# Gates of a mixing layer computed in a phase of their own, with seven products for eight

## The chip, the cores and the metric

The kernel runs on one core of a Trainium2 chip. Its time is device microseconds of one execution; the kernel before took 3154.03, 3162.03 and 3159.44 us in three runs, median 3159.44. The engines of the core are TensorE (PE; its weight loads are PEld), VectorE (DVE), ScalarE (ACT), GpSimd (POOL), and SyncE (SP), whose queue issues the DMAs in the order in which they stand in it: an issue that waits for a semaphore holds back all that stand behind it.

## The reference, cut to what matters

One decoder layer over 2048 prompt tokens and 64 sample tokens. What the change touches is the mix of three branches, each 512 wide, under gates, and the two norms behind it:

```
h = rms_norm(x, pre_mix_g)                     # 1024 wide
gate_logits = (h @ w_in)[:, 2304:]             # 3 branches x 1024
proj  = einsum('blnc,ncd->blnd', branches, w_o)
mixed = sum_n(sigmoid(gate_logits) * proj)
x1    = x + rms_norm(mixed, post_mix_g)
up    = rms_norm(x1, pre_ffn_g) @ w_up         # 1024 -> 2 x 2816, then conv, gelu, product
y     = x1 + rms_norm(act @ w_down, post_ffn_g)
```

## The kernel before

All tensors stand transposed, channels on the 128 partitions and tokens along the row. A number is kept as two float32r parts, high and low (`split`: an ACT copy, L72, and a DVE subtraction, L73), and a product of two such is three matmuls (high by high, high by low, low by high). Stage 1, to about 720 us, computes the projections and the three branches, which go to DRAM (`br`), and the norm of x by token (`rbc_d`). Stage 2 takes the 2112 tokens in three groups of 704, each of two chunks of 352 columns. It has three phases.

The mix phase (`mix_phase`) is the one that is rebuilt. Per group, `branches` goes over 3 branches x 4 steps; a step loads two tiles of gate weights (`ws_g`, 512 KB each) and one of projection weights (`ws_p`), splits them, and makes two output tiles. For each, `gemm` (L741) runs 48 matmuls for the gate (8 k-tiles x 3 passes x 2 chunks) and 24 for the projection, ACT takes the sigmoid out of PSUM (L872), DVE multiplies it with the projection (L877; L874 in the first branch, whose projections are made ahead by `proj0`), and POOL adds it to the sum (L878). At the end of a group `post_mix` takes the norm of the sum: two small PE chains (`rstd_rows`: ones against the squares, L84; a spread over the partitions, L94) with DVE, POOL and DVE between and behind, then per tile a DVE scaling (L891), a POOL addition of x (L894), a store to `x1_d` and a square, and a second such chain gives the norm of x1 (`rs2_d`). `build_h` then makes the next group's input.

Beside this, 22 calls of `prep`, one after each step, make for the up phase the four sums of weight blocks that a seven-product (Strassen) scheme needs: four loads of 256 KB (`pr`), four DVE sums (L816), four splits (`pw`), four stores of 512 KB to `sum_d`.

The up phase (`up_phase`) has 22 jobs in each of the 3 groups, and each job makes two output tiles of 704 tokens. The 2x2 blocks (two halves of the inner dimension by two output tiles, two halves by two chunks of the tokens) are multiplied with seven products of 12 matmuls each in place of eight: three with plain weight blocks (`ra`, 256 KB each), four with sums (`ws`, 512 KB each, from `sum_d`). The DVE additions that put the products together are L1031. `build_ops` makes the sums and differences of the token blocks. The down phase is not touched.

Instructions are put in order by a scheduler when the kernel is built, by priorities and pools; that order decides what stands behind a waiting instruction.

Of the kernel before, what the change touches and what calls it, by code (L numbers as in the profile page):

```python
# [9 lines left out]
F32 = mybir.dt.float32  # L10
# [5 lines left out]
P = 128  # L16
# [26 lines left out]
def tile_decoder_layer(ctx, tc, I, O):  # L43
# [8 lines left out]
    rs2_d = dpool.tile([P, NTOK], F32, tag="rs2d", name="rs2_d")  # L52
    sum_d = [dpool.tile([4, P, 2, 512], F32, tag=f"sumd{f}", name=f"sum_d{f}") for f in range(NF)]
# [46 lines left out]
    stage2(tc, I, O, br, rbc_d, x1_d, rs2_d, act_d, sum_d, gains, split, PASSES, rstd_rows)  # L100
# [609 lines left out]
def stage2(tc, I, O, br, rbc_d, x1_d, rs2_d, act_d, sum_d, gains, split, PASSES, rstd_rows):  # L710

    nc = tc.nc
    PSUM = bass.MemoryType.PSUM
    with ExitStack() as c2:

        def pool(stack, name, bufs):
            return stack.enter_context(tc.tile_pool(name=name, bufs=bufs, reuse_waits="tile"))

        cm = c2.enter_context(ExitStack())
        hp, wp, lp, sp = pool(cm, "h2", 13), pool(cm, "w2", 4), pool(cm, "ld2", 2), pool(cm, "s2", 2)  # L720

        def psum(stack, name):
            return stack.enter_context(tc.tile_pool(name=name, bufs=3, space=PSUM, reuse_waits="tile"))

        ps2 = psum(cm, "ps2")

        def load_w(src, nm):
            w = wp.tile([P, 2, 1024], F32R, tag="w", name=f"w_{nm}")
            t = lp.tile([P, 1024], F32, tag="ws", name=f"ws_{nm}", bufs=2)
            nc.sync.dma_start(out=t, in_=src)  # L730
            split(w[:, 0], w[:, 1], t)
            return w.rearrange("p s (k c) -> p s k c", c=P)

        def gemm(w, ks, xs, nm, spare=False):

            ps = ps2.tile([P, 2, 512], F32, tag="st" if spare else "mm", name=f"ps_{nm}", bufs=1 if spare else 3)
            n, tot = 0, 3 * len(xs)
            for k, x in zip(ks, xs):
                for a, b in PASSES:
                    for c in range(2):  # L740
                        nc.tensor.matmul(  # L741
                            ps[:, c, :CW], lhsT=w[:, a, k], rhs=x[:, b, c * CW : (c + 1) * CW],
                            start=(n == 0), stop=(n == tot - 1),
                        )
                    n += 1
            return ps[:, :, :CW]

        def v2(t):
            return t.rearrange("p (c n) -> p c n", c=2)

        class SumSq:


            def __init__(self, nm, nt=T2):
                self.nm, self.n, self.nt = nm, 0, nt
                self.acc = sp.tile([P, T2], F32, tag="ac", name=f"ac_{nm}", bufs=2)[:, :nt]

            def add(self, m):
                if self.n == 0:
                    nc.scalar.activation(self.acc, m, AF.Square)  # L760
                else:
                    sq = sp.tile([P, T2], F32, tag="sq", name=f"sq_{self.nm}_{self.n}", bufs=2)[:, : self.nt]
                    nc.scalar.activation(sq, m, AF.Square)
                    nc.vector.tensor_tensor(out=self.acc, in0=self.acc, in1=sq, op=ALU.add)
                self.n += 1

            def rs(self):
                psb = ps2.tile([P, 2, 512], F32, tag="st", name=f"ps_st_{self.nm}", bufs=1)
                _, self.chain = rstd_rows(
                    self.acc, self.nt, psb[:, 0, CW:], lambda c0, w: psb[:, c0 // CW, c0 % CW : c0 % CW + w], sp,  # L770
                    self.nm,
                )
                rs = sp.tile([P, T2], F32, tag="rs", name=f"rs_{self.nm}")
                nb = self.nt // CW
                nc.vector.tensor_copy(
                    out=rs[:, : self.nt].rearrange("p (c n) -> p c n", c=nb), in_=psb[:, :nb, :CW]
                )
                return rs[:, : self.nt]

        env = dict(locals())  # L780
        mix_phase(c2, tc, env)
        cm.close()
        for phase in (up_phase, down_phase):
            with ExitStack() as cs:
                env["ps2"] = psum(cs, "ps_" + phase.__name__)
                phase(c2, tc, env)


def mix_phase(c2, tc, env):

    (nc, I, br, rbc_d, x1_d, rs2_d, sum_d, gains, split, pool, hp, sp, lp, load_w, gemm, v2, SumSq) = (
        env[n] for n in (
            "nc", "I", "br", "rbc_d", "x1_d", "rs2_d", "sum_d", "gains", "split", "pool", "hp", "sp", "lp", "load_w",
            "gemm", "v2", "SumSq",
        )
    )
    with ExitStack() as ca:
        mp, ep, pp_ = pool(ca, "mx2", 13), pool(ca, "e2a", 4), pool(ca, "prep", 2)
        todo = list(range(NF))

        def prep():

            if not todo:
                return
            f = todo.pop(0)
            a = []
            for i in range(4):
                t = pp_.tile([P, 512], F32, tag="r", name=f"pr_{f}_{i}", bufs=4)
                nc.sync.dma_start(out=t, in_=I["w3"][f][:, i * 512 : (i + 1) * 512])
                a.append(t)  # L810
            a11, a12, a21, a22 = a
            for i, (o, p, m, op) in enumerate((
                (a22, a21, a22, ALU.add), (a21, a11, a21, ALU.subtract), (a11, a22, a11, ALU.subtract),
                (a12, a12, a11, ALU.subtract),
            )):
                nc.vector.tensor_tensor(out=o, in0=p, in1=m, op=op)  # L816
                w = pp_.tile([P, 2, 512], F32R, tag="pw", name=f"pw_{f}_{i}")
                split(w[:, 0], w[:, 1], o)
                nc.sync.dma_start(out=sum_d[f][i], in_=_f(w))

        def build_h(g):
            c0 = g * T2
            rb = sp.tile([P, T2], F32, tag="rbx", name=f"rbx_{g}", bufs=1)
            nc.sync.dma_start(out=rb, in_=rbc_d[:, c0 : c0 + T2])
            out = []
            for k in range(KT):
                h = hp.tile([P, 2, T2], F32R, tag="h", name=f"h_{g}_{k}")
                x = lp.tile([P, T2], F32, tag="ld", name=f"hx_{g}_{k}")
                nc.sync.dma_start(out=x, in_=I["xT"][:, k, c0 : c0 + T2])
                nc.vector.scalar_tensor_tensor(  # L830
                    out=x, in0=x, scalar=gains[:, 0, k : k + 1], in1=rb, op0=ALU.mult, op1=ALU.mult
                )
# [459 lines left out]
```

## Time and profile before

| what | value |
|---|---|
| median of three runs | 3159.44 us |
| the profiled execution | 3162.45 us |
| its span | 3160.7 us |
| PE busy in the span | 2996.0 us (95%) |
| DVE, ACT, POOL busy | 1821.8, 1329.4, 547.0 us |
| mean granted TensorE clock | 0.971 |
| moved by DMA | 566.88 MB, mean 179 GB/s |
| mix phase, about 720 to 1648 us | 928 us |

The profiled execution is 3.0 us above the median. Busy shares are means over stages with different limits, so the stages have to be read apart: the windows below do that. In them "DMA share" is the mean busy share of the core's 16 DMA engines, and PEclk is the granted TensorE clock, 1.00 being 2.4 GHz and 0.50 being 1.2 GHz.

### The profile page before, as it was taken

What the parts mean: (1) busy time and instruction counts of PE and PEld (TensorE: products, weight loads), DVE (VectorE), ACT (ScalarE), POOL (GpSimd) and SP (SyncE); (2) the same over time, 40 slices, a digit from 0 to 9 for tenths busy, and PEclk for the clock granted to TensorE, in tenths of its full rate; (3) what the DMA queues carried; (4) which work ended last, traced back from release to release, by engine and by line L of the source; (5) the groups of instructions that cost most, each with busy time, mean ns of one, the idle gap of its engine ahead of it and who ended that gap; (6) DMA issues with size and microseconds to landing.
All of it is one profiled execution on the core that took longest, in us unless ns stands there. A gap on an engine that the chain in (4) does not pass through costs nothing.

```text
span 3160.7 us, 51575 instructions
## 1 busy us (share of the span) xinstructions
PE 2996.0 (95%) x20060; PEld 2950.8 (93%) x20060; DVE 1821.8 (58%) x3061; ACT 1329.4 (42%) x2371; POOL 547.0 (17%) x662
## 2 busy tenths in 40 slices
PE   8999999998999699989994999999999997999997
PEld 8899999998999699979994999999999997999997
DVE  6665766546656832462228665865586655555552
ACT  5555565114333422332213444544454444444441
POOL 3221100000011301130113101311132210222221
PEclk9999999999999799989996999999999998999999
DMA  6222223218787832252217777777777757666652
GB/s 201 62 61 82 88 86 105 64 48 313 261 276 246 295 131 86 88 177 67 72 46 253 250 246 244 266 245 244 240 262 245 240 174 255 219 223 216 208 187 100
DMA packets 245268, 566.88 MB, mean 179 GB/s; under 512 B 30672, under 2 KB 103888, under 8 KB 245008
## 3 DMA queue, kind: packets, MB, share of 16 engines
q1 hardware_dynamic: 245024, 563.59, 53.5%
q8 instruction: 158, 2.59, 0.3%
q14 instruction: 86, 0.70, 0.1%
HBM read 459.35 MB, written 105.13 MB: 179 GB/s over the span
## 4 chain that ended last, share of the span: by engine, by line
PE 78%; DMA 8%; DVE 7%; issue 3%; ACT 2%; POOL 1%; SPq 0%; DVEq 0%; ACTq 0%; POOLq 0%
PE ps_d L1141 16%; PE ps_x L997 16%; PE ps_g L741 11%; PE ps_y L997 8%; PE ps_p L741 4%; PE ps_w L997 4%; PE ps_q L189 3%; PE ps_up L203 3%; PE ps_sv L189 3%; DMA pr<-in_w_dram 3%; PE ps_mqp L203 3%; DMA sum_d<-pw 2%; PE ps_kv L189 1%; DVE m L891 1%; DVE pw L73 1%
## 5 line engine op out<-in xcount | busy, mean ns | idle before, releaser
L741 PE MATMUL ps_g<-h,w_g 128*128 128x352 f32 x3456 | 574.1, 326 | 18.6 <-ACT m L855 18.6
L741 PEld LDWEIGHTS ps_g<-h,w_g 128*128 128x128 f32 x3456 | 566.3, 191 | 19.1 <-ACT m L855 19.1
L1141 PE MATMUL ps_d<-a,wd 128*128 128x352 f32 x3168 | 512.5, 323 | 17.8 <-ACT a L72 17.1
L1141 PEld LDWEIGHTS ps_d<-a,wd 128*128 128x128 f32 x3168 | 508.6, 189 | 19.1 <-ACT a L72 17.7
L741 PE MATMUL ps_p<-b,w_p 128*128 128x352 f32 x1728 | 291.4, 326 | 18.6 <-ACT w_p L72 13.0
L741 PEld LDWEIGHTS ps_p<-b,w_p 128*128 128x128 f32 x1728 | 283.2, 191 | 20.3 <-ACT w_p L72 13.4
L1065 DVE SCALAR_TENSOR_TENSOR c<-e,k_conv_w,c 128x704 f32<-128x704 f32 (+1 forms) x264 | 252.1, 956 | 68.8 <-ACT c L1061 61.7
L73 DVE TENSOR_TENSOR wd<-wr,wd 128x1408 fp32r<-128x1408 f32 x96 | 161.4, 1685 | 206.1 <-ACT wd L72 204.6
L997 PE MATMUL ps_x<-ot,ws 128*128 128x352 f32 x1584 | 277.5, 323 | 0.6 <-ACT p L1006 0.5
L997 PEld LDWEIGHTS ps_x<-ot,ws 128*128 128x128 f32 x1584 | 258.4, 189 | 1.9 <-ACT p L1006 1.0
L73 DVE TENSOR_TENSOR wa<-ra,wa 128x512 fp32r<-128x512 f32 x198 | 134.9, 689 | 155.5 <-ACT wa L72 154.7
L878 POOL TENSOR_TENSOR m<-m,sg 128x704 f32<-128x704 f32 x48 | 98.2, 2045 | 709.6 <-DVE sg L877 495.1
L72 ACT CAST wd<-wr 128x1408 fp32r<-128x1408 f32 x96 | 131.8, 1372 | 109.1 <-PE ps_d L1141 90.7
L872 ACT ACTIVATE sg<-ps_g 128x704 f32<-128x704 f32 x72 | 54.5, 756 | 284.4 <-PE ps_g L741 284.3
L1061 ACT ACTIVATE c<-e,k_conv_b,k_conv_w 128x704 f32<-128x704 f32 (+1 forms) x132 | 129.6, 982 | 68.8 <-DVE e L1031 49.0
L997 PE MATMUL ps_x<-ob,wa 128*128 128x352 f32 x792 | 147.3, 326 | 11.7 <-ACT wa L72 7.4
L72 ACT CAST wa<-ra 128x512 fp32r<-128x512 f32 x198 | 121.8, 624 | 85.9 <-PE ps_y L997 46.2
L73 DVE TENSOR_TENSOR w_g<-ws_g,w_g 128x1024 fp32r<-128x1024 f32 x72 | 98.7, 1371 | 91.9 <-ACT w_g L72 89.3
L1052 POOL COPY tails<-e 128x2 f32<-128x2 f32 x88 | 61.4, 697 | 520.6 <-DVE e L1031 520.4
L997 PE MATMUL ps_w<-ob,wa 128*128 128x352 f32 x792 | 147.9, 323 | 0.7 <-ACT wa L72 0.7
L997 PE MATMUL ps_y<-ot,ws 128*128 128x352 f32 x792 | 146.7, 324 | 0.3 <-DMA ws<-sum_d 0.3
L997 PEld LDWEIGHTS ps_x<-ob,wa 128*128 128x128 f32 x792 | 131.7, 191 | 12.5 <-ACT wa L72 7.6
(304 smaller groups left out, 5037.3 us busy)
## 6 DMA issues: line engine op xcount, KB each, us to landing
ws<-sum_d SPq DMA_DIRECT2D x264, 512.0 KB, 5.1
wr<-in_w_dram SPq DMA_DIRECT2D x96, 704.0 KB, 4.1
ra<-in_w_dram SPq DMA_DIRECT2D x198, 256.0 KB, 3.8
sum_d<-pw SPq DMA_DIRECT2D x88, 512.0 KB, 5.0
ws_g<-in_w_dram SPq DMA_DIRECT2D x72, 512.0 KB, 4.0
af<-act_d SPq DMA_DIRECT2D x132, 176.0 KB, 4.1
pr<-in_w_dram SPq DMA_DIRECT2D x88, 256.0 KB, 5.0
ws_p<-in_w_dram SPq DMA_DIRECT2D x36, 512.0 KB, 3.3
```

Of the source, the lines that this page charges most:

```text
L72: nc.scalar.copy(out=hi, in_=src)
L73: nc.vector.tensor_tensor(out=lo, in0=src, in1=_f(hi), op=ALU.subtract)
L189: nc.tensor.matmul(ps[:nt, :256], lhsT=h[k // 4][:, a, k % 4, c0 : c0 + nt], rhs=wv[:, b, k], start=(n == 0), stop=(n == 3 * KT - 1),)
L203: nc.tensor.matmul(ps[:, :nt], lhsT=wv[:, a, k, half * P : (half + 1) * P], rhs=h[k // 4][:, b, k % 4, :nt], start=(n == 0), stop=(n == 3 ...
L741: nc.tensor.matmul(ps[:, c, :CW], lhsT=w[:, a, k], rhs=x[:, b, c * CW : (c + 1) * CW], start=(n == 0), stop=(n == tot - 1),)
L872: nc.scalar.activation(v2(sg), ps, AF.Sigmoid)
L878: nc.gpsimd.tensor_tensor(out=mx[o], in0=mx[o], in1=sg, op=ALU.add)
L997: nc.tensor.matmul(ps[:, :CW], lhsT=self.ws[w][:, a, j], rhs=self.ops[o][j][:, b], start=(start and n == 0), stop=(n == 3 * HK - 1), skip_ ...
L1052: nc.gpsimd.tensor_copy(out=tails[:, ft], in_=e[:, T2 : T2 + 2])
L1061: nc.scalar.activation(c[:, :cwid], e[:, 2:ew], AF.Identity, bias=cb[:, ft : ft + 1], scale=cw[:, ft, 2:3])
L1065: nc.vector.scalar_tensor_tensor(out=c[:, :cwid], in0=e[:, t : t + cwid], scalar=cw[:, ft, t : t + 1], in1=c[:, :cwid], op0=ALU.mult, op1= ...
L1141: nc.tensor.matmul(ps[:, :CW], lhsT=w[:, a, k], rhs=acts[i * HF + k][:, b], start=(n == 0), stop=(n == 3 * NF - 1),)
```

## The change

The seven-product scheme of the up phase becomes a class, `Strassen`, which two phases use. A new `gate_phase` makes all gates before anything is mixed: per group 12 jobs, each two output tiles (84 matmuls, where two gate `gemm`s took 96). For group 0 the four sums of gate weights are made on DVE and stored to DRAM (12 more entries of `sum_d`); groups 1 and 2 load them. Sigmoids are taken in SBUF and stored (`sg_d`, 352 KB each, 2 per job). The 22 weight preparations for the up phase now follow the jobs of groups 1 and 2 only. The `mix_phase` that is left runs the projections, and loads the sigmoids (`sl`, five buffers). `post_mix` of a group runs inside the next group, and that of the last group after the loop. The squares of x1 are summed and stored (`acx_d`); the up phase loads them and takes the norm itself (`norms`), for group 0 ahead of its first operands, for the others during the group before. The pool for x (`xr`) has two buffers in place of four shared ones.

```
-        mix_phase(c2, tc, env)
-        cm.close()
-        for phase in (up_phase, down_phase):
...
+    for phase in (gate_phase, mix_phase, up_phase, down_phase):
...
 class Strassen:
+        def weights(self, w, sums, first, nm):
...
             for n, i in (("a11", 0), ("s1", 0), ("a12", 1), ("s2", 2), ("s4", 3), ("s3", 1), ("a22", 3)):
+                if first == "sums" and n[0] == "a":
+                    continue
+                t = wo.tile([P, 2, HK * P], F32R, tag="w", name=f"w{n}_{nm}")
+                if n[0] == "a":
+                    split(t[:, 0], t[:, 1], block(i))
+                elif first:
+                    split(t[:, 0], t[:, 1], total(i))
+                    nc.sync.dma_start(out=sums[i], in_=_f(t))
+                else:
+                    nc.sync.dma_start(out=_f(t), in_=sums[i])
...
+        def run(self, jobs):
...
+                p1 = self.copy(q, self.product(q, "x", "a11", "b11", True), "p1")
+                if prev:
+                    self.end(prev)
+                p5 = self.copy(q, self.product(q, "y", "s1", "t1", True), "p5")
+                sink.add(0, 0, p1, self.product(q, "w", "a12", "b21", True))
+                u2 = self.copy(q, self.product(q, "x", "s2", "t2", False), "u2")
+                sink.add(0, 1, u2, self.product(q, "y", "s4", "b22", False))
+                sink.half(0)
+                u3 = self.copy(q, self.product(q, "x", "s3", "t3", False), "u3")
+                sink.add(1, 1, u3, p5)
...
+def gate_phase(c2, tc, env):
...
+    op_, wo, rw = pool(c2, "ops", 32), pool(c2, "wo", 12), pool(c2, "raw", 10)
+    lp, gp, cp = pool(c2, "ldu", 3), pool(c2, "sg", 4), pool(c2, "cp", 8)
...
+        def move(self, h, c, ps):
+            nc.scalar.activation(chunk(self.sg[h], c), ps, AF.Sigmoid)
+        def half(self, h):
+            part = chunk(self.sg[h], 1) if h else self.sg[h]
+            nc.scalar.activation(part, part, AF.Sigmoid)
+            nc.sync.dma_start(out=sg_d[2 * self.i + h][:, self.g * T2 : (self.g + 1) * T2], in_=self.sg[h])
...
+            for i in range(12):
+                yield f"g{g}_{i}", eng.weights(I["wg"][i], sum_d[NF + i], g == 0, f"g{g}_{i}"), ops, Sink(g, i)
+                if g and todo:
+                    f = todo.pop(0)
+                    eng.weights(I["w3"][f], sum_d[f], "sums", f"u{f}")
...
+def mix_phase(c2, tc, env):
...
+                    sg = gp.tile([P, T2], F32, tag="sg", name=f"sl_{g}_{n}_{o}")
+                    nc.sync.dma_start(out=sg, in_=sg_d[8 * n + o][:, g * T2 : (g + 1) * T2])
...
+                if held and n == 0 and op == 1:
+                    post_mix(*held)
+                    held = None
+        held = g, mx, acc
+    post_mix(*held)
...
+    def norms(g):
+        rb = lp.tile([P, T2], F32, tag="rb", name=f"rb2_{g}", bufs=1)
+        acc = ep.tile([P, E_W], F32, tag="e", name=f"acx_{g}")
+        nc.sync.dma_start(out=acc[:, :T2], in_=acx_d[g])
+        for c in range(2):
+            psb = ps2.tile([P, 512], F32, tag="st", name=f"ps_su{g}_{c}", bufs=1)
+            cols = slice(c * CW, (c + 1) * CW)
+            rstd_rows(acc[:, cols], CW, psb[:, CW:], lambda c0, w: psb[:, c0 : c0 + w], kp, f"u{g}_{c}")
+            nc.vector.tensor_copy(out=rb[:, cols], in_=psb[:, :CW])
+        return rb
...
+                if f == 8 and g + 1 < NG2:
+                    rb = norms(g + 1)
```

Two places of SP's queue show what this moves. The first is one gate step. Before, in group 0, `pr` and `pw` are the raw blocks and split sums of a weight preparation, `ws_g` and `ws_p` the weights of gates and projections:

```order
L730 DMA ws_g0_1_30_10373<-in_w2_dram 128x1024
L819 DMA sum_d8_73<-pw_8_0_10775 128x1024
L809 DMA pr_9_0_10971<-in_w3_dram 128x512
L819 DMA sum_d8_73<-pw_8_1_10780 128x1024
L809 DMA pr_9_1_10973<-in_w3_dram 128x512
L819 DMA sum_d8_73<-pw_8_2_10785 128x1024
L809 DMA pr_9_2_10975<-in_w3_dram 128x512
L730 DMA ws_g0_1_31_10378<-in_w2_dram 128x1024
L819 DMA sum_d8_73<-pw_8_3_10790 128x1024
L809 DMA pr_9_3_10977<-in_w3_dram 128x512
L730 DMA ws_p0_1_3_10383<-in_w2_dram 128x1024
```

Now, in group 1 around job 10: `r` is a raw block and `ws` a sum, `u9` and `u10` belong to up-weight preparations, `g1_9` and `g1_10` to gate jobs, and `sg0_1_9` is the first sigmoid tile of gate job 9:

```order
L795 DMA sum_d9_76<-ws1_u9_12504 128x1024
L769 DMA r1_u9_12523<-in_w3_dram 128x512
L876 DMA sg_d18_119<-sg0_1_9_12399 128x704
L795 DMA sum_d9_76<-ws2_u9_12514 128x1024
L769 DMA r0_g1_10_12537<-in_wg_dram 128x512
L769 DMA r1_g1_10_12544<-in_wg_dram 128x512
L769 DMA r3_g1_10_12555<-in_wg_dram 128x512
L769 DMA r2_u10_12665<-in_w3_dram 128x512
L769 DMA r3_u10_12667<-in_w3_dram 128x512
L795 DMA sum_d9_76<-ws4_u9_12522 128x1024
L795 DMA sum_d9_76<-ws3_u9_12530 128x1024
L797 DMA ws1_g1_10_12541<-sum_d32_99 128x1024
```

In groups 1 and 2 a sigmoid store now stands in the queue between the loads of one job and those of the next; `sg0_1_9` is complete when the fifth product of job 9 (`s4`, the order on PE being a11, a12, s1, s2, s4, s3, a22) has been added and put through the sigmoid, and the raw blocks `g1_10` and its sums stand behind it. Before, no issue in this stretch waits for a result of PE.

The second place is the end of the mix. Before, `rb2` is the norm of x1 of group 0, `ux` are tiles of x1 for the up phase's operands, `ra` its raw weight blocks:

```order
L895 DMA x1_d2_111<-m_2_6_14217 128x704
L895 DMA x1_d2_111<-m_2_7_14244 128x704
L944 DMA rb2_0_16440<-rs2_d_64 128x704
L950 DMA ux_0_0_16442<-x1_d0_109 128x704
L950 DMA ux_0_4_16445<-x1_d0_109 128x704
L950 DMA ux_0_1_16477<-x1_d0_109 128x704
L931 DMA k_conv_w_16431<-in_conv_w_dram 128x132
L931 DMA k_conv_b_16433<-in_conv_b_dram 128x44
L931 DMA k_state_16435<-in_state_dram 128x704
L950 DMA ux_0_5_16480<-x1_d0_109 128x704
L897 DMA rs2_d_64<-rs_x12_16396 128x704
```

Now `x_u0` are the same tiles, `acx` are the summed squares:

```order
L744 DMA x_u0_1_17776<-x1_d0_147 128x704
L947 DMA x1_d2_149<-m_2_7_17018 128x704
L949 DMA acx_d2_66<-acx_2_17608 128x704
L1002 DMA k_conv_w_17703<-in_conv_w_dram 128x132
L1002 DMA k_conv_b_17705<-in_conv_b_dram 128x44
L1002 DMA k_state_17707<-in_state_dram 128x704
L769 DMA r0_u0_0_17882<-in_w3_dram 128x512
L769 DMA r1_u0_0_17889<-in_w3_dram 128x512
L769 DMA r3_u0_0_17900<-in_w3_dram 128x512
L769 DMA r0_u0_1_17999<-in_w3_dram 128x512
L769 DMA r1_u0_1_18006<-in_w3_dram 128x512
L1016 DMA acx_0_17713<-acx_d0_64 128x704
```

The load that the norm of group 0 needs, `acx_0`, has moved behind the last store of x1, the store of `acx_2`, three tables and five weight blocks, and the two chains on PE and the copies on DVE follow it; the loaded norm `rb2_0` stood right behind the stores.

On DVE the eight scalings of `post_mix` (L943 after, L891 before) stand in one block in both. In the new order the copy of the norm and the block stand between the products of a sigmoid with the projections 4 and 5 of the next group's first branch.

## Rows read from the trace of the kernel before

**Rows 1.** Windows by stage: from:to, length; busy us (instructions) by engine; PEclk, share, GB/s

```profile
720.00:1010.00 290.00, 277.25 (x1706) 276.08 (x1707) 182.59 (x224) 116.82 (x160) 29.39 (x14) 0.98 0.79 276
1010.00:1110.00 100.00, 67.25 (x392) 66.32 (x391) 81.15 (x89) 44.52 (x62) 29.81 (x12) 0.80 0.82 290
1110.00:1340.00 230.00, 230.00 (x1424) 230.00 (x1424) 76.17 (x73) 58.41 (x70) 29.68 (x15) 1.00 0.29 96
1340.00:1410.00 70.00, 54.48 (x324) 53.90 (x323) 53.60 (x48) 28.06 (x36) 25.15 (x11) 0.84 0.59 195
1410.00:1645.00 235.00, 235.00 (x1457) 235.00 (x1456) 64.03 (x59) 51.09 (x60) 29.83 (x16) 1.00 0.20 66
1645.00:1740.00 95.00, 46.89 (x245) 44.27 (x244) 69.48 (x99) 31.13 (x61) 31.03 (x16) 0.66 0.64 221
1880.00:1920.00 40.00, 40.00 (x252) 40.00 (x251) 23.95 (x33) 19.19 (x34) 3.90 (x12) 1.00 0.74 252
```

**Rows 2.** Chain of waits, inside group 1: start us, us, what

```profile
1165.91 7.76 PE ps_g L741 x48
1173.67 3.88 PE ps_p L741 x24
```

**Rows 3.** Lines by form: operation, xcount | busy us, mean ns | idle before, releasers

```profile
L741 PE MATMUL ps_g<-h,w_g 128*128 128x352 f32 x3456 | 574.1, 326 | 18.6 <-ACT m L855 18.6
...
L73 DVE TENSOR_TENSOR pw<-pr,pw 128x512 fp32r<-128x512 f32 x88 | 65.1, 745 | 37.6 <-ACT pw L72 37.5
...
L872 ACT ACTIVATE sg<-ps_g 128x704 f32<-128x704 f32 x72 | 54.5, 756 | 284.4 <-PE ps_g L741 284.3
...
L1031 DVE TENSOR_TENSOR e<-p,ps_w 128x352 f32<-128x352 f32 x66 | 34.1, 516 | 58.8 <-PE ps_w L997 58.8
```

**Rows 4.** Windows in which the DMA engines are full, columns as in the first group

```profile
720.00:740.00 20.00, 8.54 (x42) 8.54 (x43) 11.34 (x16) 7.29 (x10) 0.00 (x0) 0.66 1.02 363
...
1710.00:1720.00 10.00, 5.39 (x32) 4.81 (x31) 4.98 (x11) 2.14 (x5) 0.00 (x0) 0.92 1.04 406
1730.00:1740.00 10.00, 10.00 (x63) 9.69 (x62) 10.00 (x19) 7.11 (x15) 6.08 (x3) 1.00 1.02 359
```

**Rows 5.** Timeline, mix to up: start us, us, what [idle before <-releaser]

```profile
1643.89 4.04 PE L741 MATMUL ps_p<-b,w_p 128*128 128x352 f32 x24
...
1661.65 15.45 DVE L891 SCALAR_TENSOR_TENSOR m<-m,c_gains,rs_mix 128x704 f32<-128x704 f32 x8
...
1682.56 0.32 SPq L944 DMA_DIRECT2D rb<-rs_d  x1
...
1686.78 2.48 PE L84 MATMUL ps_st_x<-ones,ac_x 128*88 128x1 f32 x16 [26.09 <-DVE ac_x L764]
...
1689.47 1.81 DVE L951 SCALAR_TENSOR_TENSOR ux<-ux,c_gains,rb 128x704 f32<-128x704 f32 x2
...
1695.73 0.89 DVE L775 COPY rs_x<-ps_st_x 128x704 f32<-128x704 f32 x1 [0.54 <-PE ps_st_x L94]
...
1703.07 0.96 PE L997 MATMUL ps_x<-ob,wa 128*128 128x352 f32 x2 [7.38 <-ACT wa L72]
```

**Rows 6.** DMA issues: xcount, KB each, median us from issue to landing

```profile
ws<-sum_d SPq DMA_DIRECT2D x264, 512.0 KB, 5.1
...
ra<-in_w_dram SPq DMA_DIRECT2D x198, 256.0 KB, 3.8
sum_d<-pw SPq DMA_DIRECT2D x88, 512.0 KB, 5.0
...
br<-ob SPq DMA_DIRECT2D x16, 256.0 KB, 2.4
```

**Rows 7.** Timeline around the norm of group 0, columns as in the other timeline

```profile
1068.63 15.55 DVE L891 SCALAR_TENSOR_TENSOR m<-m,c_gains,rs_mix 128x704 f32<-128x704 f32 x8
...
1076.34 13.75 PE L741 MATMUL ps_g<-h,w_g 128*128 128x352 f32 x73 [10.55 <-ACT m L855]
...
1100.29 7.58 PE L741 MATMUL ps_g<-h,w_g 128*128 128x352 f32 x35
```

More of the change, by code (lines that the diff above doesn't have):

```diff
@@ L707, in pass_b, with stage2 @@
         h = hn
-def stage2(tc, I, O, br, rbc_d, x1_d, rs2_d, act_d, sum_d, gains, split, PASSES, rstd_rows):
+def stage2(tc, I, O, br, rbc_d, x1_d, acx_d, act_d, sum_d, sg_d, gains, split, PASSES, rstd_rows):
     nc = tc.nc
     PSUM = bass.MemoryType.PSUM
[L714 to L780, printed above, removed]
-        mix_phase(c2, tc, env)
-        cm.close()
-        for phase in (up_phase, down_phase):
-            with ExitStack() as cs:
-                env["ps2"] = psum(cs, "ps_" + phase.__name__)
-                phase(c2, tc, env)
@@ L945, in build_ops, with pool, v2, chunk @@
+    def pool(stack, name, bufs):
+        return stack.enter_context(tc.tile_pool(name=name, bufs=bufs, reuse_waits="tile"))
+    def v2(t):
+        return t.rearrange("p (c n) -> p c n", c=2)
+    def chunk(t, c):
+        return t[:, c * CW : (c + 1) * CW]
+    class Strassen:
+        def __init__(self, ps, op_, wo, rw, cp, lp):
+            self.pools = ps, op_, wo, rw, cp, lp
+        def operands(self, xs, nm, gain, rb):
+            _, op_, _, _, _, lp = self.pools
             ops = {n: [] for n in ("b11", "t1", "b21", "t2", "b22", "t3", "t4")}
@@ new lines, in end, with product @@
+        def end(self, q):
+            q[3].move(1, 0, self.product(q, "x", "a22", "t4", False))
+            q[3].half(1)
+        def product(self, q, bank, w, o, start):
+            nm, ws, ops, _, banks = q
+            if start:
+                banks[bank] = self.pools[0].tile(
+                    [P, 512], F32, tag="q" + bank, name=f"ps_{bank}{nm}", bufs=3 if bank == "x" else 2
+                )
+            ps, n = banks[bank], 0
+            for j in range(HK):
+                for a, b in PASSES:
+                    nc.tensor.matmul(
+                        ps[:, :CW], lhsT=ws[w][:, a, j], rhs=ops[o][j][:, b],
+                        start=(start and n == 0), stop=(n == 3 * HK - 1), skip_group_check=True,
+                    )
+                    n += 1
+            return ps[:, :CW]
@@ new lines, in copy, with __init__, add, jobs @@
+        def copy(self, q, ps, n):
+            t = self.pools[4].tile([P, CW], F32, tag="cp", name=f"{n}_{q[0]}")
+            nc.scalar.copy(out=t, in_=ps)
+            return t
+    env = dict(locals())
+    for phase in (gate_phase, mix_phase, up_phase, down_phase):
+        with ExitStack() as c2:
+            env["ps2"] = c2.enter_context(
+                tc.tile_pool(name="ps_" + phase.__name__, bufs=3, space=PSUM, reuse_waits="tile")
+            )
+            phase(c2, tc, env)
+def gate_phase(c2, tc, env):
+    nc, I, rbc_d, sum_d, sg_d, pool, ps2, Strassen, chunk = (
+        env[n] for n in ("nc", "I", "rbc_d", "sum_d", "sg_d", "pool", "ps2", "Strassen", "chunk")
+    )
+    op_, wo, rw = pool(c2, "ops", 32), pool(c2, "wo", 12), pool(c2, "raw", 10)
+    lp, gp, cp = pool(c2, "ldu", 3), pool(c2, "sg", 4), pool(c2, "cp", 8)
+    eng = Strassen(ps2, op_, wo, rw, cp, lp)
+    class Sink:
+        def __init__(self, g, i):
+            self.g, self.i = g, i
+            self.sg = [gp.tile([P, T2], F32, tag="sg", name=f"sg{h}_{g}_{i}") for h in range(2)]
+        def add(self, h, c, p, q):
+            nc.vector.tensor_tensor(out=chunk(self.sg[h], c), in0=p, in1=q, op=ALU.add)
+        def move(self, h, c, ps):
[4 more added lines that the diff above has]
+            nc.sync.dma_start(out=sg_d[2 * self.i + h][:, self.g * T2 : (self.g + 1) * T2], in_=self.sg[h])
+    def jobs():
+        todo = list(range(NF))
+        for g in range(NG2):
+            c0 = g * T2
+            rb = lp.tile([P, T2], F32, tag="rb", name=f"rb_{g}", bufs=1)
+            nc.sync.dma_start(out=rb, in_=rbc_d[:, c0 : c0 + T2])
+            ops = eng.operands(lambda k: I["xT"][:, k, c0 : c0 + T2], f"h{g}", 0, rb)
+            for i in range(12):
[3 more added lines that the diff above has]
+                    eng.weights(I["w3"][f], sum_d[f], "sums", f"u{f}")
+    eng.run(jobs())
@@ L1088, in up_phase @@
         for g in range(NG2):
[L1089 to L1090 removed]
             for f in range(NF):
[L1092 to L1099 removed]
+                yield f"u{g}_{f}", eng.weights(I["w3"][f], sum_d[f], False, f"u{g}_{f}"), ops, Sink(g, f)
@@ L1102, in down_phase @@
+                if f == 8 and g + 1 < NG2:
+                    rb = norms(g + 1)
+            if g + 1 < NG2:
+                ops = eng.operands(lambda k: x1_d[g + 1][k], f"u{g + 1}", 3, rb)
+    eng.run(jobs())
+    nc.sync.dma_start(out=O["ncv"], in_=ncv)
 def down_phase(c2, tc, env):
```

474 lines of the change are left out of this document (213 added, 261 removed).

## Prediction

> **What bounds the kernel now.** I read the windows by stage first [rows 1]. In the mix phase (about 720 to 1648 us, 928 us) TensorE sets the end: the stretches 1110:1340 and 1410:1645 are all PE, at full clock, with the DMA engines a third busy or less. The exceptions are the ends of groups: 1010:1110 has 67.25 us of PE in 100, 1340:1410 has 54.48 in 70, and 1645:1740, from the mix into the up phase, 46.89 in 95, at granted clocks of 0.80, 0.84 and 0.66. In the chain of waits a gate tile takes 7.76 us for 48 matmuls and a projection tile 3.88 for 24 [rows 2]: 0.162 us per matmul in this phase. The up phase makes 252 matmuls in 40 us, 0.159 each, at 252 GB/s and a share of 0.74 [rows 1]. Group 0 of the mix, beside which most weight preparations run, is the one long stretch of the mix with busy DMA engines: share 0.79, 276 GB/s [rows 1]. So what one reads from these rows is a PE-bound phase with three dips, and next to it a memory system with little room once transfers are dense.
>
> **The change part by part.**
>
> *Matmuls removed.* 72 gate tiles of 48 matmuls are 3456 [rows 3]; 36 jobs of 84 are 3024. The 432 fewer are worth 432 x 0.16 = 69 us if PE sets the pace, and the dips at 1010 and 1340, in which PE waits for a norm, shrink when the norm is taken beside other work. That is the gain on offer. Whether it is had depends on what a job loads.
>
> *Bytes of a gate step.* In groups 1 and 2 a job loads four sums (0.524 MB each) and three raw blocks (0.262), and stores two sigmoid tiles (0.360): 3.60 MB. Behind each of 22 of the 24 jobs stands one weight preparation: four raw loads and four stores of sums, 3.15 MB. Together 6.75 MB. The PE work of the step is 84 x 0.159 = 13.3 us, so 6.75 MB would need 507 GB/s. Where the DMA engines are full the rows have 363 and 359 GB/s, and 406 in the best 10 us [rows 4]. At 360 the volume alone takes 18.75 us. The gate step of groups 1 and 2 is therefore bound by DMA, which no stretch of the mix was.
>
> *The order of SP adds a wait.* The store of `sg0` of job n waits for that job's fifth product, its addition and its sigmoid; behind it stand the raw blocks of job n+1, stores of the preparation, and the sums of job n+1 (the order of SP's queue above). The loop is: addition 0.516 [rows 3], sigmoid 0.756 [rows 3], an issue of 0.32 (`rb`) [rows 5], and three handoffs, for which I take 0.1 each, together 1.9. Then up to the first sum of job n+1: the sigmoid store 0.360, one sum store 0.524, three raw blocks 0.786, two raw blocks of the preparation 0.524, two sum stores 1.049 and the sum itself 0.524, 3.77 MB, at 0.36 MB/us 10.5 us. Landing: a 256 KB store shows 2.4 us from issue (`br`) [rows 6], of which 0.7 is transfer, so 1.7. Then products s1, s2 and s4, 36 x 0.159 = 5.7. T = 1.9 + 10.5 + 1.7 + 5.7 = 19.8, taken as 20.0. While PE does the three products the other sums and two blocks (about 2.6 MB, 7.3 us) still flow, so the engines hardly pause, and 20.0 and the volume's 18.75 agree. By 0.315 MB/us instead of 0.36 it is 21.5; by the 406 of the best window, 18.6. DVE has eleven operations of at most 0.745 (`pw`) [rows 3] and three additions in the step, under 10 us, and hides in it; so does ACT.
>
> By the Trainium skill ("HBM Reference", section "Specifications (TRN2)") a core that streams alone gets about 425 GB/s and not its pair's share of 358; the rows with full engines lie at 359 and 363, with one at 406 [rows 4], nearer the lower. By 0.425 MB/us T would be 1.9 + 8.9 + 1.7 + 5.7 = 18.2, an estimate from that page, and the sum 40 us less.
>
> *Gates of group 0.* No preparation stands here and the sigmoid stores come two jobs late in the queue; a job moves 1.05 MB of raw blocks, 2.10 of sums stored and 0.72 of sigmoids, 3.87 MB in 13.4 us, 289 GB/s: below full. PE sets the pace: 12 x 84 x 0.16 = 161. Its start costs what the start of the up phase cost: from the first `ux` scaling at 1689.47 to 1740 [rows 5] PE made some 163 products (245 in the window less 64 small ones for the norms and 18 projections [rows 1]), 26 us of work in 50.5, a loss of 25. Before that 7 us for the first loads, and 5 for the sums that DVE makes beside the operands' splits. 198. The bounds of this: 180 (half of the start's loss) and 220 (a step of 15).
>
> *Gates of groups 1 and 2.* 22 x 20 + 2 x 13.3 + 12 for the two sets of operands, 16 loads of x among them that queue with the rest: 479.
>
> *Between gates and mix.* The first branch tiles stand behind the last sigmoid stores, as in the order of SP; the second waits for the last product. A load, a split and a weight: 10 (5 to 15).
>
> *Mix that is left.* 1728 x 0.1617 [rows 2] = 279. The DVE block of eight scalings took 15.55 us, because POOL's additions run beside it [rows 7], and the copy of the norm 0.89 [rows 5]; three PSUM buffers of 3.88 cover 11.6 of it, so PE loses about 5 and then part of a restart: after the 10.55 us gap of PE before 1076.34 and the next, 35 matmuls took 7.58 us, 0.217 each [rows 7], 1.9 us lost. 7 at each of two groups, 3 for the rest: 296. If it hides, 282; if the two x buffers draw the block out, 310.
>
> Sum: 198 + 479 + 10 + 296 = 983 against 928: +55.
>
> *Into the up phase.* Before: last projection ends at 1647.9, the scalings start at 1661.65, the load of `rb` at 1682.56, the first `ux` scaling at 1689.47, the first up product at 1703.07 [rows 5]. Group 0's norm was ready; now its squares are loaded behind the last stores of x1, and two chains on one PSUM buffer and two copies come before the first operand: about 10 (two chains of PE, DVE, POOL, PE and DVE; before, the whole chain for group 2, from the first PE chain at 1686.78 to the end of the copy at 1696.6, took 9.8 [rows 5]). x with two buffers makes the loads wait for POOL: 4. The price goes from 0, if the load passes before the tail is over, to 20. +14, and 3 for the norms of groups 1 and 2, which run under up products. The rest of the up phase and the down phase keep their order: 0.
>
> In all +72: the span 3160.7 becomes 3232.7, the execution 3162.45 becomes 3234.5. The profiled execution stands 3.0 above the median of its runs, so the forecast is **3231 us**, +2.3%. Its own range is 3205 to 3270, from T = 19 (-22) to 21.5 (+33) and a few us of the smaller terms.
>
> **The rivals.**
>
> *A, PE sets the pace of the gates.* T = 13.4, the groups 1 and 2 take 333 and not 479, and the whole ends at 3085. For it: DMA runs beside PE at 1730:1740 with PE at 10.00 of 10 [rows 4]. Against: 504 GB/s, which no window shows. Half way, with T between 14 and 16.7, lie 3099 to 3158; break-even is T = 16.7, 404 GB/s without any pause. Chance 0.12, most of it half way.
>
> *B, the clock.* If PE's wait before s1 in each step is long enough, the granted clock falls to 1.2 GHz and the three products that stand in the loop take 11.4 in place of 5.7: T = 25.7, 22 x 5.7 = 125 more, 3356. For it: the dips with clocks of 0.66 to 0.84 [rows 1] and the 0.217 us per matmul after a gap [rows 7]. Against: the step's idle time of 6 to 7 us is parted, some of it before a11, and the slower matmuls stand behind gaps of about 10 us [rows 7]. Chance 0.12.
>
> *C, faster memory:* the 406 GB/s of the best window hold throughout, T = 18.6, 3200. Against it speak the two longer or later windows at 363 and 359 [rows 4]. Chance 0.16. The Trainium skill's "HBM Reference" speaks for it; by its figure the time would be 3191.
>
> *D, no change to speak of:* small terms at their lower ends (-18 for group 0, -14 for the mix, -14 into the up phase) and T at 18.6: 3154. Chance 0.06.
>
> **How the numbers follow.** The forecast has 0.54, A 0.12, B 0.12, C 0.16, D 0.06. A measurement of this kernel tells 0.3%, 9.5 us, from no change. Faster: A's half-way cases and few of D, 0.12; same: 0.05; slower: the rest, 0.83. The range leaves out A proper and the whole of B's case: 3140 to 3315, where the upper end is B with its lower clock in two thirds of the steps.
>
> **What would show it.** Right: gate steps of groups 1 and 2 some 20 us apart, DMA share near 1.00 and 350 to 370 GB/s there, PE at about 0.67 of the stretch, `sg0` stores with SP waiting for ACT, the first `a11` idle before it, for the split of a late raw block; mix about 296 us. Wrong: a share well under 1.00 with steps of 14 (then the queue or PE decides), windows of 420 GB/s, a granted clock near 0.7 with steps above 23 (B), or a gate phase that holds while the tail or the start is what grew.

## The result, and the profile after

The changed kernel took 3242.57 us (median of four runs, 3240.3 to 3248.61) against 3159.76 (3154.03 to 3162.03): ratio 1.0268, 95% interval 1.0248 to 1.0287. The forecast was 3231 in a range of 3140 to 3315. The profiled execution has a span of 3246.8 us, 86.1 more than before; the sum had 72 more. Of the 86.1 about 3 belong to the executions that were profiled: this one stands 6.0 us above the median of its runs, the one before 3.0; by the medians the change costs 82.8.

| stretch (profile, us) | forecast | measured |
|---|---|---|
| gates of group 0, from 720 | 198 | 194 |
| gates of groups 1 and 2 | 479 | 494 |
| gates to mix | 10 | 8 |
| mix that is left | 296 | 301 |
| these four, against 928 | +55 | +69 |
| last projection to first down product, against 973.1 | +17 | +15 |
| the rest | 0 | +2 |

Windows of the changed kernel (columns as in [rows 1]): gates of group 0, gates of groups 1 and 2, the mix, and the way into the up phase.

```profile
800.00:900.00 100.00, 100.00 (x626) 100.00 (x625) 65.36 (x108) 52.32 (x106) 0.00 (x0) 1.00 0.86 298
930.00:1290.00 360.00, 274.71 (x1428) 256.82 (x1426) 168.40 (x284) 137.98 (x265) 0.00 (x0) 0.89 0.87 322
1416.00:1717.00 301.00, 292.13 (x1792) 291.29 (x1791) 219.71 (x193) 90.51 (x107) 134.50 (x65) 0.97 0.67 221
1717.00:1782.00 65.00, 12.77 (x64) 11.86 (x64) 32.53 (x31) 11.31 (x16) 22.76 (x14) 0.54 0.61 209
```

In group 0 PE works without a pause at full clock; the fifth of the seven products of each job (`s4`) starts 13.1 us after that of the job before; this distance is called a step here. In groups 1 and 2 PE is busy 275 us of 360 at a granted clock of 0.89, with the DMA engines at 0.87 and 322 GB/s. Around the change to group 1 the steps are 20.3, 9.6 and 11.5 us, then come 20 with a median of 21.6; the last, which has no preparation, is 10.2. The mix keeps PE nearly as busy as its counterpart did, 292 us of 301 [rows 1, the windows from 1110 and 1410, have all of it], and the way into the up phase has 12.77 us of PE in 65.

One step of group 1, in the timeline of the changed kernel (start us, us, what, idle before and its releaser):

```profile
1046.56 2.60 PE L832 MATMUL ps_xg<-ob_h,wa_g 128*128 128x352 f32 x12 [1.17 <-ACT wa_g L73]
...
1047.28 1.58 PEld L832 LDWEIGHTS ps_xg<-ob_h,wa_g 128*128 128x128 f32 x10 [0.43 <-DVE wa_g L74]
...
1053.38 3.65 PE L832 MATMUL ps_yg<-ot_h,ws_g 128*128 128x352 f32 x12 [2.30 <-DMA ws_g<-sum_d]
...
1060.98 0.52 DVE L868 TENSOR_TENSOR sg<-u_g,ps_yg 128x352 f32<-128x352 f32 x1 [9.35 <-PE ps_yg L832]
...
1061.54 0.79 ACT L875 ACTIVATE sg<-sg 128x704 f32<-128x704 f32 x1 [2.09 <-DVE sg L868]
...
1062.36 0.32 SPq L876 DMA_DIRECT2D sg_d<-sg  x1
...
1063.96 1.79 SPq L769 DMA_DIRECT2D r_g<-in_wg_dram  x3
...
1067.75 3.82 SPq L797 DMA_DIRECT2D ws_g<-sum_d  x4
...
1068.78 0.59 PE L832 MATMUL ps_xg<-ob_h,wa_g 128*128 128x352 f32 x2 [3.25 <-ACT wa_g L73]
...
1076.25 2.19 PE L832 MATMUL ps_yg<-ot_h,ws_g 128*128 128x352 f32 x12 [1.43 <-DMA ws_g<-sum_d]
```

It reads as the loop of the prediction. The addition behind `s4` of one job starts at 1060.98, its sigmoid at 1061.54; only then can SP issue the store `sg_d` at 1062.36, and behind that the raw blocks (1063.96) and the sums (1067.75) of the next job. Products with raw blocks start at 1068.78 and the first with a sum at 1076.25, after waits for an ACT split of a late block and for the sum itself. Between `s4`'s end and the end of the store's issue no DMA moves, and up to the first sum the engines are not quite full (windows from 1060.87 and 1062.68, columns as above):

```profile
1060.87:1062.68 1.81, 1.81 (x13) 1.63 (x11) 1.12 (x2) 1.14 (x2) 0.00 (x0) 1.00 0.00 0
1062.68:1076.25 13.57, 8.24 (x38) 7.26 (x37) 7.65 (x12) 5.64 (x11) 0.00 (x0) 0.87 0.90 322
```

SP's own waits from 960 to 1380 us (us in all, times, longest) are headed by these two, stores that wait for a sigmoid and stores that wait for a split up-weight sum:

```profile
SPq L876 <- ACT sg L875: 98.7, 16, 9.0
SPq L795 <- DVE ws_u L74: 72.2, 24, 6.0
```

PE's waits there are headed by those for the split of a late raw block, ahead of `a11`, and for a sum, ahead of `s1`:

```profile
PE ps_xg L832 <- ACT wa_g L73: 61.1, 17, 6.9
PE ps_yg L832 <- DMA ws_g<-sum_d: 22.6, 13, 3.3
```

At the end of the mix the same timeline has, where before the first up product came at 1703.07 [rows 5]:

```profile
1699.82 17.14 PE L966 MATMUL ps_p<-b,w_p 128*128 128x352 f32 x105
...
1756.39 0.43 SPq L947 DMA_DIRECT2D x_d<-m  x1
...
1763.17 0.38 SPq L1016 DMA_DIRECT2D acx<-acx_d  x1
...
1769.88 1.30 PE L85 MATMUL ps_su<-ones,acx 128*88 128x1 f32 x8 [39.72 <-DMA acx<-acx_d]
...
1775.28 1.33 PE L85 MATMUL ps_su<-ones,acx 128*88 128x1 f32 x8 [0.67 <-DVE rb L1021]
...
1780.62 2.68 DVE L745 SCALAR_TENSOR_TENSOR x_u<-x_u,c_gains,rb 128x704 f32<-128x704 f32 x3
...
1782.14 0.95 PE L832 MATMUL ps_xu<-ob_u,wa_u 128*128 128x352 f32 x2 [2.12 <-ACT ob_u L73]
```

The last projection ends at 1716.96. The last store of x1 is issued at 1756.39, the squares of group 0 at 1763.17, the two chains start at 1769.88 and 1775.28, the first scaling of a block of x1 at 1780.62 and the first up product at 1782.14: 65.2 us after the last projection, 55.1 before.

### The profile page after: what moved, and what is told of

Its sections match the earlier page's. It is cut to its first block, busy times and chain, and to the rows that moved or that the text cites. A ratio compares the mean times of both kernels' runs of the same rounds, so it can differ in the third digit from the quotient of the medians.

```text
span 3246.8 us, 52168 instructions
## 1 busy us (share of the span) xinstructions
PE 2984.2 (92%) x19628; PEld 2909.0 (90%) x19628; DVE 1961.2 (60%) x3415; ACT 1417.3 (44%) x2671; POOL 521.8 (16%) x665
## 5 line engine op out<-in xcount | busy, mean ns | idle before, releaser
L1149 PE MATMUL ps_d<-a,wd 128*128 128x352 f32 x3168 | 514.7, 324 | 17.5 <-ACT a L73 16.8
L832 PE MATMUL ps_xu<-ot_u,ws_u 128*128 128x352 f32 x1584 | 277.0, 323 | 0.2 <-ACT p_u L841 0.2
L832 PEld LDWEIGHTS ps_xu<-ot_u,ws_u 128*128 128x128 f32 x1584 | 257.5, 188 | 0.9 <-ACT p_u L841 0.5
L74 DVE TENSOR_TENSOR wa_u<-r_u,wa_u 128x512 fp32r<-128x512 f32 x198 | 135.1, 690 | 145.5 <-ACT wa_u L73 133.7
L832 PE MATMUL ps_xg<-ot_h,ws_g 128*128 128x352 f32 x864 | 152.5, 325 | 3.9 <-ACT ws_u L73 3.7
L73 ACT CAST wa_u<-r_u 128x512 fp32r<-128x512 f32 x198 | 121.8, 625 | 75.1 <-PE ps_yu L832 38.4
L832 PE MATMUL ps_wu<-ob_u,wa_u 128*128 128x352 f32 x792 | 149.4, 324 | 3.6 <-ACT ob_u L73 2.4
L832 PE MATMUL ps_xu<-ob_u,wa_u 128*128 128x352 f32 x792 | 147.2, 325 | 5.3 <-ACT ob_u L73 3.8
L832 PEld LDWEIGHTS ps_xg<-ot_h,ws_g 128*128 128x128 f32 x864 | 142.0, 190 | 4.5 <-ACT ws_u L73 4.0
L832 PE MATMUL ps_yu<-ot_u,ws_u 128*128 128x352 f32 x792 | 145.3, 324 | 0.3 <-ACT ot_u L73 0.3
L832 PE MATMUL ps_yu<-ob_u,ws_u 128*128 128x352 f32 x792 | 138.8, 322 | 0.0
```

The lines of the kernel that those rows point to most:

```text
L73: nc.scalar.copy(out=hi, in_=src)
L74: nc.vector.tensor_tensor(out=lo, in0=src, in1=_f(hi), op=ALU.subtract)
L832: nc.tensor.matmul(ps[:, :CW], lhsT=ws[w][:, a, j], rhs=ops[o][j][:, b], start=(start and n == 0), stop=(n == 3 * HK - 1), skip_group_chec ...
L1149: nc.tensor.matmul(ps[:, :CW], lhsT=w[:, a, k], rhs=acts[i * HF + k][:, b], start=(n == 0), stop=(n == 3 * NF - 1),)
```

## The experiments

All change the changed kernel, and are timed against the kernel before on the same chip; "less" is against the 3242.57 us of the changed kernel. The letters V (volume), Q (the queue's order) and others are the theories that each expectation names. The lines of the windows are the stretch 930 to 1290, whose counterpart of the changed kernel stands above (1428 matmuls, share 0.87, 322 GB/s).

**The sigmoid stores on ACT's queue.**

```
-            nc.sync.dma_start(out=sg_d[2 * self.i + h]..., in_=self.sg[h])
+            nc.scalar.dma_start(out=sg_d[2 * self.i + h]..., in_=self.sg[h])
```

> The changed kernel, but the two sigmoid stores of a gate job are issued by ACT, which makes the sigmoids, and no longer stand in SP's queue. Same bytes, same arithmetic. Its steps in groups 1 and 2 took about 20.1 us (482 us for 22 steps of 20.1, two of 13.4 and 12 for operands). Theory V (volume, 6.75 MB a step, sets the step): only the pauses of the DMA engines go, the step falls to 18.0 to 18.8 and the time by 22 x 1.3 to 2.1 = 29 to 46 us, to about 3205, DMA share in the stretch 0.95 or more. Theory Q (the queue, SP held back by the sigmoid store, sets it): the step falls to 14, the time by some 130 us to about 3110. Theory K (the half clock of the products behind a wait sets it): the step falls by under 1 us unless the waits go, 3230 or more.

3227.45 us, ratio 1.0207 (1.0192 to 1.0222): 15 less, between V and K. Steps fell to a median of 20.8.

```profile
930.00:1290.00 360.00, 278.65 (x1463) 259.84 (x1462) 172.90 (x292) 142.03 (x272) 0.00 (x0) 0.90 0.90 333
```

SP now waits at the next store in its queue, a sum of up weights that DVE has yet to split (960 to 1380 us; 72.2 before this edit):

```profile
SPq L795 <- DVE ws_u L74: 150.4, 40, 9.9
```

One wait of an in-order queue was removed, and the one behind it took over.

**Sums of gate weights made on DVE in every group.**

```
+                    if sums is not None:
                         nc.sync.dma_start(out=sums[i], in_=_f(t))
-                yield ..., eng.weights(I["wg"][i], sum_d[NF + i], g == 0, ...
+                yield ..., eng.weights(I["wg"][i], None, True, ...
```

> The changed kernel, but the four sums of gate weights are made on DVE in every group from four raw blocks; they are neither stored in group 0 nor loaded in groups 1 and 2. A step of groups 1 and 2 with a preparation moves 1.05 + 0.72 + 3.15 = 4.92 MB in place of 6.75, and DVE has 4 additions of 0.71 and 4 splits of 0.69 more, about 15 us in a step. SP still waits for the sigmoids. Theory V: 4.92 / 0.36 = 13.7, so DVE or PE decides, step 15, time 22 x 5 = 110 us less, about 3130. Theory Q: the same wait stands between the loads of two jobs and the raw blocks, sums and splits come after it, step 19 or more, about 3220 to 3240. Either way, group 0 a few us shorter.

3186.94 us, ratio 1.008 (1.0065 to 1.0095): 56 less, half of what V gave. Bytes count, but steps are about 18 and not 15:

```profile
930.00:1290.00 360.00, 301.67 (x1632) 272.97 (x1631) 277.04 (x476) 197.50 (x380) 0.00 (x0) 0.95 0.78 273
```

The DMA engines are no longer full (0.78), so volume isn't the limit here; the stores still stand in SP's queue ahead of loads, and a run below takes them out.

**Preparations spread over all 36 jobs.**

```
-                if g and todo:
+                if todo and (12 * g + i) * NF // 36 != (12 * g + i + 1) * NF // 36:
```

> The changed kernel, but the 22 weight preparations are spread evenly over the 36 gate jobs of all three groups and do not follow 22 of the last 24 jobs. Same bytes in all, same arithmetic. Theory V: 12 jobs of 3.87 MB, 24 of 3.60 and 22 preparations of 3.15 are 202 MB, 561 us at 0.36 MB/us, and with 32 for the start and the operands about 593 in place of 688: 95 us less, about 3150; with steps that stay uneven (6.75 MB with, 3.60 without) 13 of 20.1 and 11 of 13.4 in groups 1 and 2 and 7 or so of 19.5 in group 0: 22 x 6.7 less 9 x 6.7 in groups 1 and 2, plus 9 x 6 in group 0, about 35 us less, 3205. Theory Q: a step stays near 20 with or without a preparation, no gain in groups 1 and 2, and group 0 longer: 3240 or more.

3223.74 us, ratio 1.0198 (1.0181 to 1.0215): 19 less, between V with uneven steps (3205) and Q. In groups 1 and 2 the steps now alternate between about 24 and 9.6 to 18, and group 0, even before, has steps from 13 to 24. That evening out the same bytes helps little while a step can't run ahead of the next is the likely reading; it was not tested apart.

```profile
930.00:1290.00 360.00, 309.12 (x1733) 293.09 (x1733) 185.53 (x323) 156.59 (x311) 0.00 (x0) 0.93 0.90 331
```

**Both of these.**

> Both of the two: sums of gate weights made on DVE in every group with no store and no load, and the 22 preparations spread over the 36 jobs. 1.77 MB a job and 3.15 for 22 of 36, a mean of 3.70 MB, 276 GB/s at 13.4 us. Theory V: no step is bound by DMA, PE or in steps with a preparation DVE (15 us) decides; the gate phase about 32 + 36 x 13.4 to 14.5 = 515 to 555 in place of 688: time 3070 to 3110, below the kernel before. Theory Q: steps near 19, about 3230.

3144.41 us, ratio 0.995 (0.9932 to 0.9968): 0.5% faster than before, though 34 us short of V. It moves 246 GB/s:

```profile
930.00:1290.00 360.00, 328.19 (x1881) 312.46 (x1882) 290.40 (x505) 208.51 (x409) 0.00 (x0) 0.96 0.72 246
```

**All stores of the gate phase on POOL's queue**, where nothing else waits.

```
-            nc.sync.dma_start(out=sg_d..., in_=self.sg[h])
+            nc.gpsimd.dma_start(out=sg_d..., in_=self.sg[h])
-                    nc.sync.dma_start(out=sums[i], in_=_f(t))
+                    nc.gpsimd.dma_start(out=sums[i], in_=_f(t))
```

> The changed kernel, but every store of the gate phase (sigmoid tiles, sums of gate weights, sums of up weights) is issued by POOL, which has nothing else to do there; SP's queue holds loads alone. Same bytes, same arithmetic. With the sigmoid stores on ACT the time fell by 15 us only, and SP then waited for the next store in its queue: 150 us for DVE's splits between 960 and 1380 us, DMA share 0.87. Theory V: with no store in the loads' way the DMA engines stay full, share 0.97 or more, a step of 6.75 MB at 0.36 to 0.375 takes 18.0 to 18.75, the time falls by 22 x 1.4 to 2.1 = 30 to 46 us to 3197 to 3212. Theory Q (order alone): step 14, about 3110. Theory B (the twelve weight buffers that a job's seven and a preparation's four share hold back the loads): share stays at 0.87 and the time at that of the run with ACT, 3227, or above.

3196.55 us, ratio 1.0117 (1.0099 to 1.0135): 46 less, the upper end of what V said; Q falls, and so does this expectation's B (the weight buffers). With loads alone in SP's queue the engines are full, at the rate of two of the windows of [rows 4]:

```profile
930.00:1290.00 360.00, 288.19 (x1600) 263.37 (x1600) 184.77 (x314) 151.50 (x296) 61.43 (x115) 0.96 0.96 361
```

The median step is 19.5 us. POOL waits for DVE in SP's place, and nothing stands behind it that is needed (operation, xcount, busy us, mean ns, idle before and its releasers):

```profile
L795 POOL DMA_DIRECT2D sum_d<-ws_u x75 | 40.0, 533 | 151.1 <-DVE ws_u L74 147.7 <-DVE s_u L782 2.7
```

SP still waits, but now for DVE to free the buffers of raw blocks, with the engines full meanwhile (960 to 1345 us):

```profile
SPq L769 <- DVE s_u L782: 178.0, 47, 10.9
```

The granted clock of the stretch rises too, from 0.89 to 0.96; what part of the 46 us that makes was not taken apart. Nor was it tested whether a second queue as such helps, whatever its order; against it speaks the run with ACT's queue, which has a second queue as well and gained 15.

**Fewer bytes and stores on POOL.**

The edits of those two runs together.

> Sums of gate weights made on DVE in every group (4.92 MB a step in place of 6.75) and all stores of the gate phase on POOL's queue; the preparations stay behind the jobs of groups 1 and 2. Fewer bytes alone gave 56 us (3187, DMA share 0.78, 273 GB/s between 930 and 1290), stores off SP's queue alone 46 (3197, share 0.96, 361 GB/s). If bytes and queue were two separate costs, both give 102: 3140. If they are one cost seen twice (a step takes the longer of volume and queue loop), the second adds little: 3170 to 3187. If both go and DVE's 15 us a step is left: 22 x 5 = 110 less, 3130.

3150.96 us, ratio 0.997 (0.996 to 0.998): 92 less, nearly the 102 of two separate costs. Steps are 16.3, DVE is busy 304 us of 360.

```profile
930.00:1290.00 360.00, 316.84 (x1792) 291.25 (x1791) 303.83 (x518) 209.48 (x414) 68.44 (x128) 0.97 0.82 295
```

**The norm of x1 back in the mix.** `post_mix` takes the second chain and stores the norm; `norms` only loads it.

```
-        nc.sync.dma_start(out=acx_d[g], in_=acx)
+        rstd_rows(acx, T2, psx[:, 0, CW:], ..., sp, f"x1{g}")
+        nc.vector.tensor_copy(out=v2(rx), in_=psx[:, :, :CW])
+        nc.sync.dma_start(out=acx_d[g], in_=rx)
...
-            rstd_rows(acc[:, cols], CW, psb[:, CW:], ..., kp, f"u{g}_{c}")
+        nc.sync.dma_start(out=rb, in_=acx_d[g])
```

> The changed kernel, but the norm of x1 is taken in the mix phase, at the end of post_mix, as before the change; the up phase only loads it. In the changed kernel the first up product came 65.2 us after the end of the last projection, before 55.1. Theory of the prediction: the late load of the squares and two chains ahead of the first operand cost about 10, so 10 to 14 us come back, 3229 to 3233. Rival: the start of the up phase waits for weights and blocks of x1 that are loaded behind the stores anyway, and the chains in the next group cost PE a few us: 3240 to 3245.

3242.49 us, ratio 1.026 (1.0244 to 1.0277): no difference, as the rival said. The way into the up phase is shorter, 57.7 us in place of 65.2 from the last projection's end (1724.53) to the first up product:

```profile
1699.80 24.73 PE L972 MATMUL ps_p<-b,w_p 128*128 128x352 f32 x152
...
1782.26 2.11 PE L832 MATMUL ps_xu<-ob_u,wa_u 128*128 128x352 f32 x6
```

But the mix is longer, 311 us in place of 301, since the chain runs among the projections on PE, 1.41 and 1.91 us in each of two groups, and adds work to DVE and ACT there; group 1 has

```profile
1576.38 1.41 PE L85 MATMUL ps_sx<-ones,acx 128*88 128x1 f32 x16 [1.02 <-DVE acx L929]
...
1584.41 1.91 PE L95 MATMUL ps_sx<-ident,rstd_x 88*128 88x88 f32 x16
```

So the late norm does cost 7.5 us at the end, but the mix saves about as much by it; what makes the 3 us beyond PE's 6.6 was not taken apart.

**The norm of the sum at the end of its own group.**

```
-                if held and n == 0 and op == 1:
-                    post_mix(*held)
-                    held = None
-        held = g, mx, acc
-    post_mix(*held)
+        post_mix(g, mx, acc)
```

> The changed kernel, but the norm of the sum and what follows it stand at the end of their own group in the program and not in the middle of the next group's first branch. If the place in the program matters, PE waits about 13 us more at each of two ends of groups: 3265. If the scheduler brings the next group's projections forward by itself (it does put five of its tiles ahead of the chain's second half), the time is the same within 5 us: 3238 to 3248.

3247.29 us, ratio 1.0272 (1.0253 to 1.029): the same within the intervals. The scheduler brings the next group's projections forward whichever way it is written: here too projections of group 1 stand on PE between and behind the two parts of the chain of group 0 (timeline from 1510 us).

```profile
1509.77 12.13 PE L966 MATMUL ps_p<-b,w_p 128*128 128x352 f32 x74
...
1521.74 1.34 PE L85 MATMUL ps_st<-ones,ac 128*88 128x1 f32 x16
1522.94 5.31 PE L966 MATMUL ps_p<-b,w_p 128*128 128x352 f32 x32
...
1528.09 1.92 PE L95 MATMUL ps_st<-ident,rstd_mix 88*128 88x88 f32 x16
1529.80 12.53 PE L966 MATMUL ps_p<-b,w_p 128*128 128x352 f32 x76
```

**All that helped.** Sums remade, preparations spread, stores on POOL, norm in the mix:

> Sums of gate weights made on DVE in every group, preparations spread over the 36 jobs, stores of the gate phase on POOL's queue, norm of x1 in the mix phase: all parts that the runs so far or the theory V say help. The run with the first two took 3144 with PE at 97% in its best stretch and 89% in others. If queue waits made the rest: another 20 us for the stores, 10 for the norm: 3110 to 3120. If DVE is what holds the steps with a preparation (15 us of its work in 13.4 of PE): 3130 to 3140.

3118.47 us, ratio 0.9867 (0.9852 to 0.9882): faster than both kernels, by 1.3% than the one before. Most steps are 13.4 to 16.8, PE runs 1986 matmuls in the stretch:

```profile
930.00:1290.00 360.00, 332.83 (x1986) 322.12 (x1986) 298.42 (x514) 215.93 (x426) 58.00 (x108) 0.98 0.75 263
```

With the norm in the up phase instead:

> As the fastest kernel so far (3118, sums remade, preparations spread, stores on POOL), but with the norm of x1 in the up phase as in the change. By the run that moved the norm alone (no difference) this is the same within 5 us: 3114 to 3123. If the norm's place mattered once the gate phase is short: 3128 or more.

3121.78 us, ratio 0.988 (0.9857 to 0.9904), the same within the intervals.

## Why the prediction was right

*The gates of groups 1 and 2 are bound by DMA and its queue, not by PE.* Right, and the two halves of the step's price were nearly separable: with the bytes unchanged and no store in SP's queue the engines fill (361 GB/s against 322) and 46 us go; with fewer bytes 56 go; with both, 92. One sign of the prediction failed: it had the engines hardly pausing, at a share near 1.00 and 350 to 370 GB/s, with PE at 0.67 of the stretch. Measured were 0.87, 322 and 0.76. Volume alone did not set the step; the pauses that the queue makes came on top.

*Rivals A and C.* A needed 504 GB/s; no stretch came near. C needed 406 throughout; the run with its stores on POOL has 361 over 360 us, though shorter windows of it are higher, here 390:

```profile
1140.00:1190.00 50.00, 42.06 (x239) 39.33 (x237) 24.46 (x42) 20.20 (x40) 8.24 (x16) 0.97 1.02 390
```

By the Trainium skill ("HBM Reference", "Specifications (TRN2)") a core alone gets about 425 GB/s; no run here shows that over a long stretch.

*T = 20.0* was mis-sized by a little: the median of the 20 long steps is 21.6. From the end of `s4` to the end of the store's issue they take 1.8 us in the median (1.9 forecast), from there to the product with the first sum 13.8 (12.2), and the three products 6.0 (5.7). The term that was too small is the second: the prediction let 0.36 MB/us flow, and the window from 1062.68 above has 322 GB/s, with SP's waits at sum stores in it. The prediction's own variant at 0.315 MB/us gave 21.5.

*The total of 494 for groups 1 and 2 is helped by luck.* The 20 long steps took 440 us, where 20 of T are 400. The four others, the operands within them, took 51.6, where the forecast had 78.6 (two of T, two of 13.3, and 12): the first jobs of group 1 came 9.6 and 11.5 us apart, which nothing in the prediction says and whose cause stays open.

*Rival B, the clock,* was a part of the truth and not a case of its own. The twelve matmuls at 1053.38 took 3.65 us in place of 2.08, and the granted clock there was at the lower level; those at 1046.56 took 2.60 at full clock, held up by a late split of their weights (the weight load at 1047.28 above; window lines as before):

```profile
1046.56:1049.15 2.59, 2.45 (x13) 2.16 (x14) 1.73 (x3) 1.72 (x4) 0.00 (x0) 1.00 1.03 388
1053.38:1057.03 3.65, 3.65 (x14) 3.65 (x15) 0.00 (x0) 0.00 (x0) 0.00 (x0) 0.56 1.00 381
```

The three products that stand in the loop lost about 10 us to it over the 20 long steps, some 1.6 us in each of six. The raw-block products before them ran at 1.2 GHz more often, but in 13 of the steps `s1` then still waited for its sum, so that little of this can show in the time; in the other steps it was not taken apart.

*The gain was on offer but was spent.* 432 fewer matmuls are 69 us at 0.16 each. Group 0 shows the pace, 13.1 us for 84 matmuls where two gate tiles took 15.5 [rows 2]; groups 1 and 2 lost it to DMA. The run with all that helped is 42.7 us below the kernel before.

*Group 0, start and mix* stand within 5 us of their terms. The block of eight scalings, 7 us forecast per group, is in the trace of the changed kernel (12.86 us of DVE, and a wait of PE of 4.40 at its end):

```profile
1536.42 12.86 DVE L943 SCALAR_TENSOR_TENSOR m<-m,c_gains,rs 128x704 f32<-128x704 f32 x8
...
1550.23 15.95 PE L966 MATMUL ps_p<-b,w_p 128*128 128x352 f32 x84 [4.40 <-DVE m L975]
```

*Into the up phase* the sum had 14 and 3, the trace 10 to the first product and 5 behind it, which were not taken apart. The step named the late load of the squares and the chains; both are there. That the norm in the mix would be no cheaper in all was not foreseen by the prediction.

*The place of `post_mix` in the program* was counted as a gain at the ends of groups; undone, it changes nothing. The dips of before [rows 1, from 1010 and 1340] are gone; that the gates, which needed the next group's input there, made them is likely and was not tested.

## What to carry to other kernels

Before counting saved matmuls, count the bytes of one step of the new phase and divide by the rate of windows whose DMA engines are full; work that was spread beside a long PE phase can make the bound of a shorter one. In an in-order DMA queue a store that waits for a result holds back every load behind it: put such stores on the queue of an idle engine, and expect the next wait in line when only one is taken away. Such waits do no harm by themselves: the kernel before had 94.6 us of them between 720 and 1010, at its stores of sums, while PE was busy 277 us of 290 [rows 1]. They cost time where the loads behind them are needed at once, as in the loop here.

```profile
SPq L819 <- DVE pw L73: 94.6, 56, 7.9
```

A piece that is moved to where it looks free may cost there what it saved here.

## What had not been expected

Stores issued by POOL cost little: in the run with all of them there an issue takes POOL 533 ns, where the same stores of up-weight sums took SP 376 in the median, and POOL has the time. The half clock came without a long single wait: in the step above PE had pauses of 1.2 and 2.3 us, and most of the dozen behind the second ran at 1.2 GHz.
